# Attention scores in split precision: three 64-row matmuls per map, two maps in turn, instead of two 128-row matmuls on stacked parts

## The chip, the cores and the metric

The kernel runs on one core of a Trainium2 chip. A core has five engines that run side by side: TensorE (matrix products, PE in the profile, with its weight loads as PEld), VectorE (DVE), ScalarE (ACT), GpSimd (POOL) and SyncE (SP), whose queue issues nearly all DMA transfers here. The metric is the device time of one execution in microseconds (us); lower is better. Shown are the times of three runs and one profiled execution.

## The reference

One layer of a residual trunk on 2048 positions of width 1024, in float32:

```
u = rms_norm(h);  proj = u @ W_in            # diff q,k,v | sb q,k,v
# diff attention, 4 heads, two maps c = 0, 1 of 64 columns each, QK-normed
logits = einsum('bqhcd,bkhcd->bhcqk', q, k) * scale + bias   # chunk-causal mask
p = softmax(logits);  attn = p[:, :, 0] - lam * p[:, :, 1];  y_A = attn @ v
# stick-breaking attention, 8 heads of 64 columns, strictly causal
z = einsum('bqhd,bkhd->bhqk', q, k) * scale
log_1mb = where(mask, log_sigmoid(-z), 0)
rem = cumsum(log_1mb, reverse) - log_1mb
a = where(mask, exp(log_sigmoid(z) + rem), 0);  y_B = a @ v
h = h + concat(norm(y_A), norm(y_B)) @ W_out
h = h + (silu(u2 @ W_gate) * (u2 @ W_up)) @ W_down,  u2 = rms_norm(h)
```

Everywhere the contraction of a score is over 64 columns of q and k.

## The kernel before

Every float32 operand of a product is split into a high and a low float16 part, and a product is summed from high x high, high x low and low x high. The work has two parts. The first (pools `ps`, `sp`, `zp`, `pp`) holds the input projection, both attentions and the output projection; the second is the feed-forward network, whose products over blocks are formed in a scheme with seven products.

The first part runs over eight groups `g` of 128 query columns: `g` 0 to 3 are the diff heads, one head with its two maps each; `g` 4 to 7 are the stick-breaking heads, two heads each. "Map" below means either, `m` = 0 or 1; a map has 64 columns. For each group the projection (`proj`, `proj_tile` L315, 24 matmuls of 384 columns for each of 16 row tiles) gives q, k and v of that group. After every four row tiles `proj_batch` (L349) puts q and k, split, into the float16 tile `st` and turns them by DMA into `qT` and `kT`, with positions along the free axis. In `st` the high and low 64 columns of one map lie next to each other, so that after the transpose a map's high part lies on partitions 0 to 63 and its low part on 64 to 127, 128 rows in all. Two more DMAs (L375) copy the two planes of `qT` with the halves exchanged, low above high, into its planes 0 and 1.

Scores are formed for one row tile `i` of 128 queries and up to 512 keys at a time (a chunk), in a PSUM tile `sc` of one bank; there are four such banks. `score_chunk` (L447) issues two matmuls of 128 rows, 128 columns of output partitions and 128 to 512 moving columns: the first gives high x high + low x low, the second, with the exchanged plane, low x high + high x low. For the last chunk of the stick-breaking heads a third one (L451) adds the mask.

In the diff heads `probs` (L463) goes through map 0 and then map 1: VectorE takes each chunk from PSUM to a float32 tile `z4`, with scaling and a running maximum (L484, and L488 with the bias near the diagonal). Then come the exponentials (ScalarE), the combination of both maps (L508), and `split_t` (L399), which splits into float16 halves and transposes by DMA into `aT` for the product with v (`pv`, L454).

In the stick-breaking heads `stage_a` (L541) treats one map of up to 1024 keys: for each chunk, from the last to the first, two sigmoids on ScalarE (L555 into the tile `om`, L556 in place in PSUM), on VectorE a running product from right to left (L558, a scan) and a product (L559) into the tile `be`, and at the end `split_t` of `be`, its high part on ScalarE and its low part on GpSimd (L99). `stage_b` (L566), some units later, forms the product with v. The tiles `om` and `be` come from the pool of nine `z4` tiles (`ZB` = 9); the float16 tiles before and after the transpose come from rings of three and five.

The order in which an engine executes is not that of the source. A scheduler puts the instructions in order, by priorities (`PRI`, L32) and by when their inputs and buffers come free in its own timeline; matmuls of the projection for the next group, of the products with v and of the scores so stand mixed in TensorE's queue. The projection is advanced (`advance`, L709) by the progress of the attention.

`xf` in `out_proj` (L748) uses the buffers of `st` later for rows of x.

Of the kernel before, what the change touches and what calls it, by code (L numbers as in the profile page):

```python
# [11 lines left out]
F32 = mybir.dt.float32  # L12
F16 = mybir.dt.float16
# [47 lines left out]
def block(tc, a, out):  # L61
# [3 lines left out]
    with top:  # L65
# [185 lines left out]
        with ExitStack() as ph1:  # L251
# [82 lines left out]
            @pri("po")  # L334
            def proj_out(g, G, pj, B, j):
                st, v, raw = B
                nv = 1 if g < 4 else 2
                vv = v[:, j, :].rearrange("p (h s e) -> p h s e", h=nv, s=2)
                split_psum(vv[:, :, 0, :], vv[:, :, 1, :], pj[:, 256:384].rearrange("p (h e) -> p h e", h=nv), 128)
                if g < 4:  # L340
                    if pick(A=270, D=335) == "A":
                        ACT.mul(raw[:, j, :], pj[:, :256], 2.0 ** -11)
                    else:
                        DVE.tensor_scalar(raw[:, j, :], pj[:, :256], 2.0 ** -11, None, op0=ALU.mult)
                else:
                    split_psum(st[:, 0:4, j, 0, :], st[:, 0:4, j, 1, :], pj[:, :256].rearrange("p (c e) -> p c e", c=4), 256)

            @pri("pb")
            def proj_batch(g, G, B):  # L349
                st, v, raw = B  # L350
                qT = sp.tile([P, 4, 4, P], F16, tag="qT", bufs=QB, name=nm("qT"))
                kT = sp.tile([P, 2, 4, P], F16, tag="kT", bufs=KB, name=nm("kT"))
                if g < 4:
                    rq = raw[:].rearrange("p t (c e) -> p t c e", e=64)
                    sq = st[:].rearrange("p c t s e -> p (c t s e)")[:, :2048].bitcast(F32)
                    ACT.activation(sq.rearrange("p (t c e) -> p t c e", t=4, c=4), rq, AF.Square)
                    note("A", 950)
                    ss = sm.tile([P, 16], F32, tag="ss", bufs=2, name=nm("ss"))
                    DVE.tensor_reduce(ss[:], sq.rearrange("p (c e) -> p c e", e=64), op=ALU.add, axis=AX.X)
                    rs = sm.tile([P, 16], F32, tag="rs", bufs=2, name=nm("rs"))  # L360
                    rstd(rs[:], ss[:], 2.0 ** -16 / 64, G["epsk"][:])
                    rsb = rs[:].rearrange("p (t c) -> p t c", c=4).unsqueeze(3).to_broadcast([P, 4, 4, 64])
                    DVE.tensor_tensor(rq, rq, rsb, ALU.mult)
                    note("D", 2300)
                    gb = gk[:].unsqueeze(1).unsqueeze(1).to_broadcast([P, 4, 2, 64])
                    tt(rq[:, :, 2:4, :], rq[:, :, 2:4, :], gb, ALU.mult, 512)
                    for o in range(2):
                        src = rq[:, :, 2 * o : 2 * o + 2, :]
                        d = st[:, 2 * o : 2 * o + 2].rearrange("p c t s e -> p t c s e")
                        to16(d[:, :, :, 0, :], src, 512)  # L370
                        tt(d[:, :, :, 1, :], src, d[:, :, :, 0, :], ALU.subtract, 512)
                for T, c in ((qT[:, 2:4], 0), (kT[:], 2)):
                    SP.dma_start_transpose(T.rearrange("p c t n -> p (c t) n"), st[:, c : c + 2].rearrange("p c t s e -> p (c t s e)"))
                for o in (0, 64):
                    SP.dma_start(qT[o : o + 64, 0:2].rearrange("p c t n -> p (c t n)"), qT[64 - o : 128 - o, 2:4].rearrange("p c t n -> p (c t n)"))  # L375
                G["q"].append(qT)
                G["k"].append(kT)
                G["v"].append(v)

            def proj(g, G, fresh=None):  # L380
                for t in range(NT):
# [62 lines left out]
                return (i % k, k)  # L444

            @pri("sc")
            def score_chunk(G, sc, i, q, m, w, cut=False):  # L447
                for o in range(2):
                    PE.matmul(sc[:, : 128 * w].rearrange("p (t n) -> p t n", n=P), lhsT=G["q"][i // 4][:, 2 - 2 * o + m, i % 4, :], rhs=G["k"][q][:, m, 0:w, :], start=o == 0, stop=o == 1)  # L449
# [11 lines left out]
            def diff_attn(g, G):  # L461
                @pri("at")
                def probs(i):  # L463
# [8 lines left out]
                    for m in range(2):  # L472
                        nx = 0
                        for b in range(nb):
                            n = min(1024, L - 1024 * b)
                            z = z4()
                            for c in range((n + 511) // 512):
                                lo, hi = 512 * c, min(512 * c + 512, n)
                                sc = ps.tile([P, 512], F32, tag="sc", bufs=4, name=nm("sc"))
                                score_chunk(G, sc, i, 2 * b + c, m, (hi - lo) // P)  # L480
                                f = min(max(near - 1024 * b - lo, 0), hi - lo)
                                note("D", 1.05 * (hi - lo) + 200)
                                if f > 0:
                                    DVE.tensor_scalar(z[:, lo : lo + f], sc[:, :f], kz_d[:], None, op0=ALU.mult, op1=ALU.max, accum_out=mx[:, m, nx : nx + 1])  # L484
                                    nx += 1
                                if f < hi - lo:
                                    b0 = 1024 * b + lo + f - (i - 1) * 128
                                    DVE.tensor_tensor_reduce(z[:, lo + f : hi], sc[:, f : hi - lo], bias[:, g, b0 : b0 + hi - lo - f], kz_d[:], -3.0e38, ALU.add, ALU.max, mx[:, m, nx : nx + 1])  # L488
                                    nx += 1
                            zs[m].append((b, n, z))  # L490
# [46 lines left out]
            def sb_attn(g, G):  # L537
                last = {}

                @pri("at")  # L540
                def stage_a(i, m, b):  # L541
                    L = (i + 1) * 128
                    n = min(1024, L - 1024 * b)
                    be, om = z4(), z4()
                    if b == i // 8:
                        DVE.memset(om[:, n : n + 1], 8192.0)
                    else:
                        DVE.tensor_copy(om[:, n : n + 1], last[m][:, 0:1])
                    last[m] = om
                    for c in range((n - 1) // 512, -1, -1):  # L550
                        lo, hi = 512 * c, min(512 * c + 512, n)
                        w = hi - lo
                        sc = ps.tile([P, 512], F32, tag="sc", bufs=4, name=nm("sc"))
                        score_chunk(G, sc, i, 2 * b + c, m, w // P, b == i // 8 and hi == n)
                        ACT.activation(om[:, lo:hi], sc[:, :w], AF.Sigmoid, scale=G["nkz"][:])  # L555
                        ACT.activation(sc[:, :w], sc[:, :w], AF.Sigmoid, scale=G["kz"][:])  # L556
                        ov = om[:, lo:hi][:, ::-1]
                        DVE.tensor_tensor_scan(ov, ov, sc[:, :w], om[:, hi : hi + 1], op0=ALU.mult, op1=ALU.bypass)  # L558
                        DVE.tensor_tensor(be[:, lo:hi], sc[:, :w], om[:, lo + 1 : hi + 1], ALU.mult)  # L559
                        note("A", 1.7 * w + 400)  # L560
                        note("D", 3.15 * w + 350)
                    return n, split_t(be[:, :n], n, "A", "P")

                ypd = {}

# [177 lines left out]
            def out_proj():  # L743
                for t in range(NT):
                    mt = pp.tile([P, 2 * D], F16, tag="xt", bufs=3, name=nm("mt"))[:].rearrange("p (k n) -> p k n", k=KT)
                    with tc.high_priority(PRI["wm"]) if PRI["wm"] else nullcontext():
                        mts.append(SP.dma_start(mt, ms[t]))
                    xf = pp.tile([P, 6, 4, 2, 64], F16, tag="st", name=nm("xf"))[:].rearrange("p c t s e -> p (c t s e)").bitcast(F32)[:, :D]  # L748
# [425 lines left out]
```

## Time and profile before

| | |
|---|---|
| Runs before, median (lowest to highest) | 2856.76 us (2854.7 to 2862.01) |
| Profiled execution: its own time | 2849.59 us |
| Profiled execution: span from the first to the last instruction | 2847.8 us |
| Mean granted TensorE clock | 0.957 |
| Score matmuls (L449) | 1280, 347.2 us busy, first and last at about 105 and 1391 us |
| Projection matmuls (L321) | 3072, 576.2 us busy |
| Products with v (L459) | 4896, 281.3 us busy |
| Transfers that exchange the halves of qT (L375) | 64 of 128 KB |

A group of instructions is shown as line, engine, operation, written tile <- read tiles, shapes and count, then its busy time and the mean of one in ns, then the time its engine sat idle just before it and what ended that. A row of busy times by stretch gives the stretch, its length, the busy time and count of each engine, the granted TensorE clock, the share of the DMA engines and GB/s. A timeline row gives start and length in us, engine, line, and how many instructions of a kind followed one another; the length runs to the end of the last one's record. Matmul ends are modelled, and matmuls overlap, so a sum of record lengths is more than the time they took. In the waits, "A <- B" is the time that A sat idle until B released it, with the number of waits and the longest.

### The profile page before, as it was taken

To read this page: it belongs to the slowest core of one execution; us is meant where nothing else is said; L and a number is where in the kernel's file an instruction comes from. 1 tells how busy PE (TensorE), PEld (TensorE's weight loads), DVE (VectorE), ACT (ScalarE), POOL (GpSimd) and SP (SyncE) were. 2 spreads that over 40 slices of the span, in tenths; PEclk is the share of its full clock that TensorE was granted. 3 is DMA by queue.
4 is the path that set the end of the run, shared out by engine and by line. 5 is a ranking of instruction groups with operands and counts; after the bars stand their busy time and mean duration, and the time that the engine had idled before them with its cause. 6 is when DMAs were issued, how large, how long until landed. Compare 5 with 4: busy or idle time off the path is not lost.

```text
span 2847.8 us, 45790 instructions
## 1 busy us (share of the span) xinstructions
PE 2519.3 (88%) x17052; PEld 1409.9 (50%) x17052; DVE 2229.5 (78%) x3922; ACT 1481.5 (52%) x2666; POOL 1703.5 (60%) x1133
## 2 busy tenths in 40 slices
PE   7998898888888777788888999899998999999997
PEld 4565556555555444477763444444443444444443
DVE  6898879787989999787638776877778868678675
ACT  4665656567787888656515443534433324334231
POOL 3577767664545545455627655656666667576663
PEclk9999999999999888999989999999999999999998
DMA  7778887889999898978876434242336442442424
GB/s 235 191 160 177 169 176 168 172 166 219 215 193 197 161 182 162 204 168 226 213 255 181 144 107 163 73 149 97 125 133 238 132 163 84 151 165 74 148 74 177
DMA packets 680094, 469.07 MB, mean 165 GB/s; under 512 B 520688, under 2 KB 610800, under 8 KB 678080
## 3 DMA queue, kind: packets, MB, share of 16 engines
q1 hardware_dynamic: 678048, 464.08, 63.1%
q8 instruction: 133, 2.18, 0.3%
q0 software_dynamic: 512, 1.36, 0.2%
q10 hardware_dynamic: 1312, 0.72, 0.1%
q14 instruction: 89, 0.73, 0.1%
HBM read 239.32 MB, written 90.96 MB: 116 GB/s over the span
## 4 chain that ended last, share of the span: by engine, by line
PE 21%; DVE 16%; DMA 7%; POOL 6%; issue 5%; ACT 3%; SPq 1%; DVEq 0%; POOLq 0%; ACTq 0%
PE pd L1008 11%; DVE wu L215 3%; PE pd L911 3%; POOL fst L99 3%; PE pm L911 3%; PE pa L911 3%; DVE wd L215 2%; DVE cg L99 2%; DMA fst<-in_w_down_dram 2%; DVE cg L976 1%; PE po L757 1%; DVE z L558 1%; DMA aT<-s 1%; DMA xcd<-b 1%; DMA b<-b 1%
## 5 line engine op out<-in xcount | busy, mean ns | idle before, releaser
L99 POOL TENSOR_TENSOR s<-z,s 128x1024 f16<-128x1024 f32 (+7 forms) x288 | 474.5, 1656 | 327.8 <-ACT s L90 299.5
L321 PE MATMUL pj<-w,xt 128*128 128x384 f16 x3072 | 576.2, 336 | 25.7 <-DVE st L331 9.6
L99 POOL TENSOR_TENSOR fst<-fst 128x512 f32<-128x512 f32 x193 | 348.3, 1805 | 225.2 <-DVE wg L215 98.0
L1008 PE MATMUL pd<-wd,act 128*128 128x512 f16 x1848 | 416.2, 384 | 30.0 <-DVE hs L1017 11.2
L321 PEld LDWEIGHTS <-xt 128*128 128x128 f16 x3072 | 301.4, 100 | 238.2 <-issue 45.0
L558 DVE TENSOR_TENSOR_SCAN z<-z,sc 128x512 f32<-128x512 f32 (+3 forms) x320 | 355.6, 1113 | 74.8 <-ACT sc L556 70.6
L449 PE MATMUL sc<-kT,qT 128*128 128x512 f16 (+3 forms) x1280 | 347.2, 362 | 72.7 <-DVE z L559 26.3
L459 PE MATMUL yp<-v,aT 128*128 128x64 f16 (+1 forms) x4896 | 281.3, 207 | 77.1 <-DMA aT<-s 76.2
L459 PEld LDWEIGHTS <-aT 128*128 128x128 f16 x4896 | 244.8, 101 | 168.6 <-DMA aT<-s 105.4
L911 PEld LDWEIGHTS <-wg 128*128 128x128 f16 x1848 | 185.8, 101 | 279.3 <-issue 76.2
L1008 PEld LDWEIGHTS <-act 128*128 128x128 f16 x1848 | 181.4, 99 | 256.6 <-issue 25.0
L911 PEld LDWEIGHTS <-wu 128*128 128x128 f16 x1848 | 182.1, 99 | 231.7 <-issue 19.2
L99 POOL TENSOR_TENSOR hs<-hs,cu 128x512 f32<-128x512 f32 x138 | 190.6, 1391 | 165.4 <-DVE cu L1017 66.4
L90 ACT CAST s<-z 128x384 f16<-128x384 f32 (+7 forms) x216 | 170.4, 790 | 139.2 <-DMA aT<-s 59.0
L1017 DVE SCALAR_TENSOR_TENSOR hs<-pd,c,hs 128x512 f32<-128x512 f32 x192 | 139.0, 745 | 131.0 <-PE pd L1008 98.6
L99 POOL TENSOR_TENSOR act<-cg,act 128x512 f16<-128x512 f32 x108 | 173.2, 1609 | 103.1 <-ACT act L970 103.1
L555 ACT ACTIVATE z<-sc,c 128x512 f32<-128x512 f32 (+3 forms) x320 | 203.8, 637 | 20.4 <-PE sc L449 10.5
L559 DVE TENSOR_TENSOR z<-sc,z 128x512 f32<-128x512 f32 (+3 forms) x320 | 193.3, 606 | 7.7
L556 ACT ACTIVATE sc<-sc,c 128x512 f32<-128x512 f32 (+3 forms) x320 | 196.0, 613 | 0.0
L757 PE MATMUL po<-wo,mt 128*128 128x256 f16 x1536 | 184.2, 279 | 13.0 <-DVE xf L760 12.5
L970 ACT CAST act<-cg 128x512 f16<-128x512 f32 x132 | 80.5, 615 | 212.1 <-DVE cg L976 124.8
L911 PE MATMUL pm<-X,wg 128*128 128x512 f16 x792 | 178.6, 379 | 1.0 <-POOL wg L214 1.0
(228 smaller groups left out, 4480.8 us busy)
## 6 DMA issues: line engine op xcount, KB each, us to landing
xt<-xs SPq DMA_DIRECT2D x112, 512.0 KB, 4.2
hs<-hd SPq DMA_DIRECT2D x96, 512.0 KB, 4.3
hd<-hs SPq DMA_DIRECT2D x80, 512.0 KB, 5.1
fst<-in_w_gate_dram SPq DMA_DIRECT2D x22, 1024.0 KB, 5.1
fst<-in_w_up_dram SPq DMA_DIRECT2D x22, 1024.0 KB, 5.3
fst<-in_w_down_dram SPq DMA_DIRECT2D x22, 1024.0 KB, 4.8
X<-xcd SPq DMA_DIRECT2D x14, 1024.0 KB, 9.6
wst<-in_w_in_dram SPq DMA_DIRECT2D x24, 512.0 KB, 6.5
```

The costliest lines, as they stand in the source:

```text
L90: ACT.copy(dst, src)
L99: (DVE if e == "D" else POOL).tensor_tensor(dst, a_, b_, op)
L321: PE.matmul(pj[:, :384], lhsT=xv[:, xi, kt, :], rhs=G["w"][:, wi, kt, :], start=n == 0, stop=n == 23)
L449: PE.matmul(sc[:, : 128 * w].rearrange("p (t n) -> p t n", n=P), lhsT=G["q"][i // 4][:, 2 - 2 * o + m, i % 4, :], rhs=G["k"][q][:, m, 0:w, ...
L459: PE.matmul(yp[:, y0 : y0 + wd], lhsT=aT[:, a_, :], rhs=v[:, v_ : v_ + wd], start=start and j == 0 and q == 0, stop=stop and j == nb - 1 a ...
L555: ACT.activation(om[:, lo:hi], sc[:, :w], AF.Sigmoid, scale=G["nkz"][:])
L556: ACT.activation(sc[:, :w], sc[:, :w], AF.Sigmoid, scale=G["kz"][:])
L558: DVE.tensor_tensor_scan(ov, ov, sc[:, :w], om[:, hi : hi + 1], op0=ALU.mult, op1=ALU.bypass)
L559: DVE.tensor_tensor(be[:, lo:hi], sc[:, :w], om[:, lo + 1 : hi + 1], ALU.mult)
L757: PE.matmul(po[:, sl], lhsT=mt[:, kt, P * xi : P * xi + P], rhs=wos[2 * h + n][wi][:, kt, :], start=q == 0, stop=q == 23)
L911: PE.matmul(ps_[:].rearrange("p (t n) -> p t n", n=P), lhsT=wv[:, wo, wi, 128 * kt : 128 * kt + 128], rhs=X[xo][:, :, xi, kt, :], start=st ...
L1008: PE.matmul(po[:], lhsT=act[:, ao, xi, 128 * j : 128 * j + 128], rhs=W["d"][:, wo, wi, :], start=start and u == 0 and q == 0, stop=u == nu ...
```

## The change

Scores are formed by three matmuls of 64 rows for each map: high q x high k, low q x high k, high q x low k. The product low x low is no longer formed. For this, `st` now has four planes, q high, q low, k high and k low, each with both maps side by side, 64 columns each. After the transpose map 0 lies on partitions 0 to 63 and map 1 on 64 to 127 in each plane. `qT` has two planes in place of four, and the DMAs that exchanged its halves are gone. `score_pair` takes two score tiles, one for each map, and issues the three products for the two maps in turn, one on the lower and one on the upper half of the partitions. `probs` and `stage_a` ask for both maps of a chunk at once and treat them one after the other; `stage_a` splits both maps at its end. Sizes of pools and rings are as they were.

```diff
                 else:
-                    split_psum(st[:, 0:4, j, 0, :], st[:, 0:4, j, 1, :], pj[:, :256].rearrange("p (c e) -> p c e", c=4), 256)
+                    split_psum(st[:, 0:4:2, j, :], st[:, 1:4:2, j, :], pj[:, :256].rearrange("p (c e) -> p c e", c=2), 256)
...
-                qT = sp.tile([P, 4, 4, P], F16, tag="qT", bufs=QB, name=nm("qT"))
+                qT = sp.tile([P, 2, 4, P], F16, tag="qT", bufs=QB, name=nm("qT"))
...
                     for o in range(2):
-                        src = rq[:, :, 2 * o : 2 * o + 2, :]
-                        d = st[:, 2 * o : 2 * o + 2].rearrange("p c t s e -> p t c s e")
-                        to16(d[:, :, :, 0, :], src, 512)
-                        tt(d[:, :, :, 1, :], src, d[:, :, :, 0, :], ALU.subtract, 512)
-                for T, c in ((qT[:, 2:4], 0), (kT[:], 2)):
-                    SP.dma_start_transpose(T.rearrange("p c t n -> p (c t) n"), st[:, c : c + 2].rearrange("p c t s e -> p (c t s e)"))
-                for o in (0, 64):
-                    SP.dma_start(qT[o : o + 64, 0:2].rearrange("p c t n -> p (c t n)"), qT[64 - o : 128 - o, 2:4].rearrange("p c t n -> p (c t n)"))
+                        src = raw[:, :, 128 * o : 128 * o + 128]
+                        to16(st[:, 2 * o], src, 512)
+                        tt(st[:, 2 * o + 1], src, st[:, 2 * o], ALU.subtract, 512)
+                for T, c in ((qT, 0), (kT, 2)):
+                    SP.dma_start_transpose(T[:].rearrange("p s t n -> p (s t) n"), st[:, c : c + 2].rearrange("p c t e -> p (c t e)"))
...
-                        st = pp.tile([P, 6, 4, 2, 64], F16, tag="st", name=nm("st"))
+                        st = pp.tile([P, 4, 4, P], F16, tag="st", name=nm("st"))
...
             @pri("sc")
-            def score_chunk(G, sc, i, q, m, w, cut=False):
-                for o in range(2):
-                    PE.matmul(sc[:, : 128 * w].rearrange("p (t n) -> p t n", n=P), lhsT=G["q"][i // 4][:, 2 - 2 * o + m, i % 4, :], rhs=G["k"][q][:, m, 0:w, :], start=o == 0, stop=o == 1)
+            def score_pair(G, i, q, w, cut=False):
+                sc = [ps.tile([P, 512], F32, tag="sc", bufs=4, name=nm("sc")) for _ in range(2)]
+                for n, (a_, b_) in enumerate(((0, 0), (1, 0), (0, 1))):
+                    for m in range(2):
+                        h = slice(64 * m, 64 * m + 64)
+                        PE.matmul(sc[m][:, : 128 * w].rearrange("p (t n) -> p t n", n=P), lhsT=G["q"][i // 4][h, a_, i % 4, :], rhs=G["k"][q][h, b_, 0:w, :], start=n == 0, stop=n == 2)
                 if cut:
-                    PE.matmul(sc[:, 128 * w - P : 128 * w], lhsT=idb[:], rhs=tri[:], start=False, stop=True, skip_group_check=True)
+                    for m in range(2):
+                        PE.matmul(sc[m][:, 128 * w - P : 128 * w], lhsT=idb[:], rhs=tri[:], start=False, stop=True, skip_group_check=True)
+                return sc
...
                 @pri("at")
-                def stage_a(i, m, b):
+                def stage_a(i, b):
                     L = (i + 1) * 128
                     n = min(1024, L - 1024 * b)
-                    be, om = z4(), z4()
...
+                    u = [(z4(), z4()) for _ in range(2)]
...
-                        sc = ps.tile([P, 512], F32, tag="sc", bufs=4, name=nm("sc"))
-                        score_chunk(G, sc, i, 2 * b + c, m, w // P, b == i // 8 and hi == n)
...
-                    return n, split_t(be[:, :n], n, "A", "P")
+                        scs = score_pair(G, i, 2 * b + c, w // P, b == i // 8 and hi == n)
+                        for (be, om), sc in zip(u, scs):
...
+                    return n, [split_t(be[:, :n], n, "A", "P") for be, _ in u]
...
                     for b in range(i // 8, -1, -1):
+                        n, aTs = stage_a(i, b)
                         for m in range(2):
-                            n, aT = stage_a(i, m, b)
-                            pend.append((i, m, b, n, aT))
+                            pend.append((i, m, b, n, aTs[m]))
```

In `probs` the loop over the maps moves inside the loop over chunks in the same way.

More of the change, by code (lines that the diff above doesn't have):

```diff
@@ L471, in probs @@
                     mx = sm.tile([P, 2, 8], F32, tag="mx", name=nm("mx"))
[L472 to L478, printed above, removed]
-                                sc = ps.tile([P, 512], F32, tag="sc", bufs=4, name=nm("sc"))
-                                score_chunk(G, sc, i, 2 * b + c, m, (hi - lo) // P)
-                                f = min(max(near - 1024 * b - lo, 0), hi - lo)
+                    nx = 0
+                    for b in range(nb):
+                        n = min(1024, L - 1024 * b)
+                        z = [z4() for _ in range(2)]
+                        for c in range((n + 511) // 512):
+                            lo, hi = 512 * c, min(512 * c + 512, n)
+                            sc = score_pair(G, i, 2 * b + c, (hi - lo) // P)
+                            f = min(max(near - 1024 * b - lo, 0), hi - lo)
+                            k = nx
+                            for m in range(2):
+                                nx = k
                                 note("D", 1.05 * (hi - lo) + 200)
                                 if f > 0:
-                                    DVE.tensor_scalar(z[:, lo : lo + f], sc[:, :f], kz_d[:], None, op0=ALU.mult, op1=ALU.max, accum_out=mx[:, m, nx : nx + 1])
+                                    DVE.tensor_scalar(z[m][:, lo : lo + f], sc[m][:, :f], kz_d[:], None, op0=ALU.mult, op1=ALU.max, accum_out=mx[:, m, nx : nx + 1])
                                     nx += 1
@@ L487, in probs @@
                                     b0 = 1024 * b + lo + f - (i - 1) * 128
-                                    DVE.tensor_tensor_reduce(z[:, lo + f : hi], sc[:, f : hi - lo], bias[:, g, b0 : b0 + hi - lo - f], kz_d[:], -3.0e38, ALU.add, ALU.max, mx[:, m, nx : nx + 1])
+                                    DVE.tensor_tensor_reduce(z[m][:, lo + f : hi], sc[m][:, f : hi - lo], bias[:, g, b0 : b0 + hi - lo - f], kz_d[:], -3.0e38, ALU.add, ALU.max, mx[:, m, nx : nx + 1])
                                     nx += 1
-                            zs[m].append((b, n, z))
+                        for m in range(2):
+                            zs[m].append((b, n, z[m]))
                     ng = sm.tile([P, 2], F32, tag="ng", name=nm("ng"))
@@ L747, in out_proj @@
                         mts.append(SP.dma_start(mt, ms[t]))
-                    xf = pp.tile([P, 6, 4, 2, 64], F16, tag="st", name=nm("xf"))[:].rearrange("p c t s e -> p (c t s e)").bitcast(F32)[:, :D]
+                    xf = pp.tile([P, 4, 4, P], F16, tag="st", name=nm("xf"))[:].rearrange("p c t e -> p (c t e)").bitcast(F32)
                     SP.dma_start(xf, x[t * P : (t + 1) * P, :])
```

28 lines of the change are left out of this document (14 added, 14 removed).

## The prediction

> **What bounds the kernel now.** I read the page's busy times first, then the busy times by stretch. The attention part, in which the changed matmuls lie, runs from about 105 us, the first score matmul, to 1410 us. I cut it at 610 us: the stick-breaking heads ("sb") begin there with their first scan, and before it lie the softmax heads ("diff").
>
> ```profile
> PE 2519.3 (88%) x17052; PEld 1409.9 (50%) x17052; DVE 2229.5 (78%) x3922; ACT 1481.5 (52%) x2666; POOL 1703.5 (60%) x1133
> ...
> core 0: us, PE busy (x) PEld busy (x) DVE busy (x) ACT busy (x) POOL busy (x), PEclk, DMA share, GB/s
> 100.00:200.00 100.00, 95.95 (x729) 60.32 (x728) 90.40 (x289) 64.21 (x173) 64.15 (x50) 1.00 0.80 177
> 105.00:610.00 505.00, 457.19 (x3622) 292.04 (x3620) 431.57 (x1300) 304.78 (x795) 354.39 (x253) 0.98 0.80 172
> 610.00:1410.00 800.00, 657.70 (x6768) 446.48 (x6766) 673.85 (x1177) 587.25 (x1102) 429.98 (x281) 0.93 0.91 192
> ...
> L449 PEld LDWEIGHTS <-qT x1280: 95/98/152, 105.5 to 1390.9; 128*128 128x128 f16 x183
> L558 DVE TENSOR_TENSOR_SCAN z<-z,sc x320: 455/1271/1281, 613.4 to 1396.1; 128x512 f32<-128x512 f32 x88, 128x128 f32<-128x128 f32 x24, 128x256 f32<-128x256 f32 x24, 128x384 f32<-128x384 f32 x24
> ```
>
> In the diff stretch TensorE is busy 457 of 505 us (90%) and idle 48; in its best 100 us it reaches 96%. In the sb stretch it is busy 658 of 800 (82%) and idle 142, and VectorE is a little busier than it (674, 84%). So the first stretch is TensorE's, the second is shared. Next I read what the score matmuls are, by shape, and how tightly TensorE's runs stand in the timeline (start, length, what).
>
> ```profile
> L449 PE MATMUL sc<-kT,qT 128*128 128x512 f16 x896 | 277.4, 394 | 49.9 <-DVE z L559 22.5 <-DVE z L546 11.5 <-DVE z L548 9.3
> L449 PE MATMUL sc<-kT,qT 128*128 128x384 f16 x128 | 33.7, 347 | 5.7 <-DVE z L548 2.8 <-DVE z L546 2.7
> L449 PE MATMUL sc<-kT,qT 128*128 128x256 f16 x128 | 25.5, 284 | 6.3 <-DVE z L546 2.8 <-DVE z L548 2.1 <-DVE z L559 1.2
> L449 PE MATMUL sc<-kT,qT 128*128 128x128 f16 x128 | 20.3, 226 | 10.9 <-DMA kT<-st 3.0 <-DMA qT<-qT 2.7 <-DVE z L559 2.6
> ```
>
> ```profile
> 184.17 0.39 PE L459 MATMUL yp<-v,aT 128*128 128x128 f16 x4
> 184.39 0.38 PE L449 MATMUL sc<-kT,qT 128*128 128x256 f16 x2
> 184.61 0.55 PE L459 MATMUL yp<-v,aT 128*128 128x128 f16 x7
> ...
> 186.57 0.59 PE L449 MATMUL sc<-kT,qT 128*128 128x512 f16 x2
> 187.00 1.46 PE L321 MATMUL pj<-w,xt 128*128 128x384 f16 x8
> 188.30 0.59 PE L449 MATMUL sc<-kT,qT 128*128 128x512 f16 x2
> ...
> 193.00 0.49 PE L449 MATMUL sc<-kT,qT 128*128 128x384 f16 x2
> 193.32 1.14 PE L321 MATMUL pj<-w,xt 128*128 128x384 f16 x6
> ```
>
> A matmul's record (394 ns) is longer than the time it takes from its neighbours: from 186.57 to 187.00 two 512-column ones cost 0.43 us, 0.215 each; 384 columns cost 0.16, 256 columns 0.11, and 128 columns 0.055 (four from 184.17 to 184.39). Weight loads cost nothing beside them. Each record also overlaps the next run by about 0.16 us (186.57 + 0.59 = 187.16, next run at 187.00): the array drains one while it takes in the next.
>
> **The change, part by part.** *The score stream.* Now it is 896 x 0.215 + 128 x (0.16 + 0.11 + 0.055) = 193 + 42 = 234 us, 117 in each stretch (the two kinds of head have the same chunks). The change makes it three matmuls of the same columns in place of two: one after another they take 351 us, +117. They take less only where two on different halves (partitions 0 to 63, 64 to 127) stand next to each other and run side by side. The source alternates the halves, but the instructions are put in order by a scheduler, and in the changed kernel's order on TensorE they mostly do not alternate. The 1920 matmuls stand in 527 runs with other work between them, 246 in diff and 281 in sb, and 456 of the runs are just the three of one map. Only 289 neighbours in all change the half. Letting the second of such neighbours start with the first, as its half is free, saves 32 us over all runs (20 in diff, 12 in sb). So the stream grows by 85 us at least and 117 at most. No row here shows two halves side by side; I take the middle, 101 (49 diff, 52 sb).
>
> By the Trainium skill, TensorE: Matmul & The Clock Gate, Part 3 (Packing small matmuls), matmuls in distinct row groups do run at the same time; by that rule the growth would be 85, and with strict alternation the stream would even shrink to three quarters, about -59 us.
>
> *Changing the array between 128 and 64 rows.* Every run now sits between matmuls of 128 rows, so TensorE's array form changes 2 x 527 = 1054 times, 492 in diff and 562 in sb. The profile has three such excursions, for the bias table's 32-row matmuls; the one at full clock, and for comparison another f32 run that keeps 128 rows:
>
> ```profile
> 32.94 0.67 PE L321 MATMUL pj<-w,xt 128*128 128x384 f16 x3
> 33.55 0.91 PE L634 MATMUL bt<-z,z 32*128 32x384 f32 x2
> 34.38 0.34 PE L321 MATMUL pj<-w,xt 128*128 128x384 f16 x1
> ...
> 761.86 0.60 PE L432 MATMUL yp<-id,y 128*128 128x128 f32 x4
> 762.29 0.65 PE L321 MATMUL pj<-w,xt 128*128 128x384 f16 x3
> ```
>
> Going in, the record before ends at 33.61 and the run starts at 33.55, an overlap of 0.06 in place of 0.16: 0.10 us lost. Going out, 34.46 against 34.38: 0.08 lost. The f32 run of 128 rows overlaps its successor by 0.17, so it is the rows and not the type. At 0.09 each, 1054 changes cost 95 us (44 diff, 51 sb). The bounds are 0, if 64 rows do not behave as 32, and 0.10 each, 105 us. I take 95, the only row there is.
>
> The Trainium skill, TensorEngine Tiling (Array Packing), Key Properties, says that a change of tiling mode drains TensorE, and does not limit that to 32 rows; by it the bound of 0 falls.
>
> *What TensorE's added time does to the end.* Added are 93 us in diff and 103 in sb. Diff: 457 + 93 = 550 us of work in a stretch that is packed to 90% and at best to 96%. At 93%, halfway, it takes 592, so +87. Sb: 658 + 103 = 761; at 96% it would still fit in 800, at today's 82% it would take 926. VectorE holds a bound of its own there, and idle time beside it can fill; I take 92%, which is 827, so +27. Sum +114. The FFN from 1410 us on has no part in the change.
>
> *The swapped copy of q.* Its plane is dropped, and with it 64 transfers on SP's queue:
>
> ```profile
> qT<-qT SPq DMA_DIRECT2D x64, 128.0 KB, 2.5
> ...
> L375 SPq DMA_DIRECT2D qT<-qT x64: 461/587/1224, 75.0 to 1217.2; - x64
> ...
> who waited for it (us, times):
>   PE sc L449: 2.9, 5
>   PEld L449: 2.7, 3
> ```
>
> They hold SP's queue for 64 x 0.59 = 38 us, and TensorE waited for them 5.6 us in all. Between 0 and 6 us of gain; I count 0, since the q transpose before them stays. The transposes stay as many and as large. The new layout of `st` moves no instruction to another engine.
>
> *Two maps in turn.* Score tiles of both maps are requested together, and `stage_a` builds both maps before it splits either, so the splits and their transposes come in twos, and four `z4` tiles are taken at once from a ring of nine. What stands in the way of this today:
>
> ```profile
> L99 POOL TENSOR_TENSOR s<-z,s 128x1024 f16<-128x1024 f32 x120 | 264.5, 2208 | 163.7 <-ACT s L90 148.2 <-issue 6.8 <-DVE m L178 4.2
> L558 DVE TENSOR_TENSOR_SCAN z<-z,sc 128x512 f32<-128x512 f32 x224 | 285.0, 1273 | 40.6 <-ACT sc L556 38.0 <-PE pj L321 1.6
> L559 DVE TENSOR_TENSOR z<-sc,z 128x512 f32<-128x512 f32 x224 | 153.4, 686 | 5.1
> ...
> POOL s L99 <- ACT s L90: 299.5, 136, 11.4
> DVE z L558 <- ACT sc L556: 70.6, 58, 6.8
> ```
>
> VectorE needs 2 x 2 x (1.27 + 0.69) = 7.8 us for a 1024-wide block of both maps, GpSimd 2 x 2.2 = 4.4 for its two splits: one block's splits are done while VectorE does the next. Counted at 0, hidden under those 7.8 us; without that cover it is a rival below, on the one side, and the 70.6 us for which the scan waits for ScalarE are one on the other.
>
> *Sum.* The profiled execution took 2849.6 us (span 2847.8). 2849.6 + 114 = 2964; it lies 7 us under the median of the runs, 2856.8, so the median to expect is 2971, 4% slower.
>
> **The rivals.**
> 1. *TensorE has room.* The halves overlap where they can, changing rows is free, and the rest goes into idle time. Diff: 457 + 39 = 496, at 96% 517, so +12; sb: 658 + 46 = 704 in 800, +0. 2857 + 12 = 2869. For it: 48 + 142 us of idle. Against it: the 0.08 and 0.10 us above.
> 2. *Faster: the scan stops waiting.* With two independent maps in turn, ScalarE has the second map's sigmoids ready while VectorE scans the first, and the 70.6 us before the scan vanish: 2857 - 71 = 2786. It decides only if TensorE's added time is under what it has idle, 190 us, and is issued in time; at my 196 it does not. Against it: diff has no such wait to give back and is TensorE's.
> 3. *The ring makes the blocks wait.* A block's first `om` tile reuses a `be` tile of two blocks earlier, so it waits for that one's split; before, the slack was three maps, now two. GpSimd is busy only 430 of 800 us in sb, but it already waits 299.5 us for ScalarE's half of the split, and ScalarE does that behind its sigmoids. There are 24 blocks in each of four sb groups; if each loses half a split, 1.1 us, that is 96 x 1.1 = 106 us on top: 3077.
>
> **How the numbers follow.** The forecast, 2971, has 0.66; its own bounds are the stream at 85 to 117 and the changes at 0 to 105, with the packing between today's and the best, from rival 1's 2869 to (457 + 59 + 49) / 0.905 = 624 (+119) and (658 + 59 + 56) / 0.822 = 940 (+140) on top of 2857, 3116. Rival 1 has 0.07, of which 0.04 lie within 0.3% (9 us, about what a measurement of this kernel tells from no change) and 0.03 a little above. Rival 2 has 0.06, rival 3 0.21. So faster 0.06, same 0.04, slower 0.90. I cut the range where a tenth is left out on either side: 2880 to 3085.
>
> **What will show it.** In the changed profile: 1920 score matmuls of 64 rows; a start-to-start time of 0.215 us within a run of three of one map; an overlap of records of some 0.07 where a run begins and ends; TensorE's idle share in attention below today's; attention's end near 1520 us with the FFN's length unchanged; the waits for score tiles (VectorE's at L484, ScalarE's at L555) grown. The forecast is wrong if the runs of 64 rows keep the 0.16 us overlap, if matmuls of one half are much shorter than 0.215, or if VectorE's queue rather than TensorE's carries the longer attention.

## The result

The changed kernel takes 2931 us against 2856 us: the ratio is 1.025 (95% interval 1.023 to 1.028), 75 us slower, 4 runs each. The prediction said slower, 2971 us, with 2880 to 3085 as its range: the sign and the range held, and of the forecast's 114 us came 75. Its profiled execution took 2925.6 us (span 2923.6).

To see where the time went I cut each kernel's execution by events: first score matmul, first scan (end of the diff heads), last scan, end. For the kernel before these are at 106, 613, 1396 and 2848 us. For the changed kernel they are read from two lines of the views by line, first and last start:

```profile
L449 PEld LDWEIGHTS <-qT x1920: 92/94/148, 105.0 to 1461.2; 64*128 64x128 f16 x192
L563 DVE TENSOR_TENSOR_SCAN z<-z,sc x320: 451/1270/1282, 661.7 to 1463.5; 128x512 f32<-128x512 f32 x112, 128x128 f32<-128x128 f32 x16, 128x256 f32<-128x256 f32 x16, 128x384 f32<-128x384 f32 x16
```

Busy times by stretch: stretch, its length, then PE, PEld, DVE, ACT, POOL, the granted clock, DMA share, GB/s. First before:

```profile
106.00:613.00 507.00, 459.19 (x3664) 294.33 (x3663) 434.06 (x1305) 307.43 (x799) 354.71 (x254) 0.98 0.80 172
613.00:1396.00 783.00, 642.12 (x6554) 432.43 (x6552) 665.32 (x1162) 578.39 (x1089) 417.60 (x273) 0.93 0.91 191
1396.00:2848.00 1452.00, 1334.22 (x6384) 630.75 (x6381) 1055.43 (x1295) 544.97 (x676) 891.80 (x560) 0.96 0.43 144
```

and after:

```profile
105.00:662.00 557.00, 524.67 (x3917) 277.80 (x3916) 435.75 (x1298) 305.00 (x794) 353.57 (x253) 0.99 0.68 150
662.00:1464.00 802.00, 735.49 (x6937) 437.81 (x6936) 667.79 (x1171) 580.76 (x1094) 418.14 (x273) 0.93 0.88 184
1464.00:2924.00 1460.00, 1333.60 (x6390) 630.94 (x6386) 1053.22 (x1293) 545.94 (x677) 891.66 (x559) 0.96 0.43 143
```

The diff stretch is 50 us longer, the sb stretch 19, the rest 8. VectorE, ScalarE and GpSimd do the same work in both. TensorE is busy 65 us more in diff, which is then packed to 94% (91% before), and 93 us more in sb, packed to 92% (82% before). So most of the added work in diff lengthened it, and most of that in sb went into idle time.

The score matmuls in the groups, and TensorE's timeline (start, length, line, count):

```profile
L449 PE MATMUL sc<-kT,qT 64*128 64x512 f16 (+3 forms) x1920 | 423.9, 362 | 46.5 <-DVE z L564 25.2
```

```profile
179.82 2.60 PE L321 MATMUL pj<-w,xt 128*128 128x384 f16 x15
182.35 1.48 PE L449 MATMUL sc<-kT,qT 64*128 64x512 f16 x12
183.76 0.95 PE L461 MATMUL yp<-v,aT 128*128 128x128 f16 x14
184.65 0.82 PE L449 MATMUL sc<-kT,qT 64*128 64x512 f16 x3
185.40 0.40 PE L461 MATMUL yp<-v,aT 128*128 128x128 f16 x4
185.73 0.50 PE L449 MATMUL sc<-kT,qT 64*128 64x256 f16 x3
```

The group's busy time rose from 347 to 424 us, by 77. But it counts each run to the end of its last record, with the overlap into the next run and the change of rows behind it, so it is not the stream of the prediction. Counted in the trace from each start to the next, with idle time left out, the score matmuls took 259 us before and 389 after, of which the 527 changes behind their runs are 49: the stream grew by 82 us, 33 in diff and 49 in sb. Twelve matmuls that alternate between the halves took 1.41 us from start to next start (182.35 to 183.76), where twelve in a row at 0.215 would take 2.6: two on different halves do run side by side (six pairs at 0.215 are 1.29, and the change of rows behind them 0.09). A run of three of one map took 0.75 (184.65 to 185.40): 3 x 0.215 and 0.10 more, the change behind it. Each record overlaps its neighbour by 0.06 to 0.07 us where the rows change (183.76 + 0.95 = 184.71 against 184.65; 185.47 against 185.40) and not by 0.16: the 0.09 us per change that the 32-row rows of before gave. Over all runs the median change costs 0.092 us on leaving (308 ns from a 512-column matmul to the next start, in place of 216) and 0.095 us on entering (258 ns after a projection matmul, in place of 163).

### The profile page after: what moved, and what is told of

It is laid out like the page before. It is cut to its first block, busy times and chain, and to the rows that moved or that the text cites. A ratio compares the mean times of both kernels' runs of the same rounds, so it can differ in the third digit from the quotient of the medians.

```text
span 2923.6 us, 47071 instructions
## 1 busy us (share of the span) xinstructions
PE 2676.2 (92%) x17692; PEld 1398.6 (48%) x17692; DVE 2230.3 (76%) x3922; ACT 1482.8 (51%) x2666; POOL 1706.1 (58%) x1133
## 4 chain that ended last, share of the span: by engine, by line
PE 26%; DVE 17%; DMA 8%; POOL 6%; issue 5%; ACT 3%; SPq 0%; DVEq 0%; POOLq 0%; ACTq 0%
PE pd L1013 11%; PE pd L916 3%; PE po L762 3%; DVE wu L215 3%; POOL fst L99 3%; PE pa L916 2%; PE pm L916 2%; DVE z L563 2%; DVE wd L215 2%; DMA aT<-s 2%; DVE cg L99 2%; PE sc L449 2%; DMA fst<-in_w_down_dram 1%; DVE cg L981 1%; DMA hs<-hd 1%
## 5 line engine op out<-in xcount | busy, mean ns | idle before, releaser
L99 POOL TENSOR_TENSOR s<-z,s 128x1024 f16<-128x1024 f32 (+7 forms) x288 | 468.6, 1638 | 325.0 <-ACT s L90 268.1
L321 PE MATMUL pj<-w,xt 128*128 128x384 f16 x3072 | 567.8, 332 | 15.1 <-DMA xt<-xs 5.2
L449 PE MATMUL sc<-kT,qT 64*128 64x512 f16 (+3 forms) x1920 | 423.9, 362 | 46.5 <-DVE z L564 25.2
L563 DVE TENSOR_TENSOR_SCAN z<-z,sc 128x512 f32<-128x512 f32 (+3 forms) x320 | 353.1, 1111 | 80.2 <-ACT sc L561 74.5
L321 PEld LDWEIGHTS <-xt 128*128 128x128 f16 x3072 | 288.3, 99 | 245.6 <-issue 76.5
L461 PEld LDWEIGHTS <-aT 128*128 128x128 f16 x4896 | 226.7, 101 | 151.6 <-issue 93.0
L560 ACT ACTIVATE z<-sc,c 128x512 f32<-128x512 f32 (+3 forms) x320 | 204.1, 638 | 41.4 <-PE sc L449 21.8
L449 PEld LDWEIGHTS <-qT 64*128 64x128 f16 x1920 | 119.9, 96 | 207.9 <-issue 64.9
L487 DVE TENSOR_SCALAR_CACHE_REDUCE z<-sc,c 128x512 f32<-128x512 f32 (+3 forms) x256 | 161.7, 649 | 49.6 <-PE sc L449 45.3
```

The source lines that it names most:

```text
L99: (DVE if e == "D" else POOL).tensor_tensor(dst, a_, b_, op)
L321: PE.matmul(pj[:, :384], lhsT=xv[:, xi, kt, :], rhs=G["w"][:, wi, kt, :], start=n == 0, stop=n == 23)
L449: PE.matmul(sc[m][:, : 128 * w].rearrange("p (t n) -> p t n", n=P), lhsT=G["q"][i // 4][h, a_, i % 4, :], rhs=G["k"][q][h, b_, 0:w, :], st ...
L461: PE.matmul(yp[:, y0 : y0 + wd], lhsT=aT[:, a_, :], rhs=v[:, v_ : v_ + wd], start=start and j == 0 and q == 0, stop=stop and j == nb - 1 a ...
```

## The experiments

Each ran beside the kernel before on the same chip; times are medians, ratios are to that kernel with their 95% intervals.

**pairs: the handling of two maps alone.** The changed kernel with the layout, the copies and the 128-row matmuls of before:

```diff
-                for n, (a_, b_) in enumerate(((0, 0), (1, 0), (0, 1))):
-                    for m in range(2):
-                        h = slice(64 * m, 64 * m + 64)
-                        PE.matmul(sc[m]..., lhsT=G["q"][i // 4][h, a_, i % 4, :], rhs=G["k"][q][h, b_, 0:w, :], start=n == 0, stop=n == 2)
+                for m in range(2):
+                    for o in range(2):
+                        PE.matmul(sc[m]..., lhsT=G["q"][i // 4][:, 2 - 2 * o + m, i % 4, :], rhs=G["k"][q][:, m, 0:w, :], start=o == 0, stop=o == 1)
```

> The changed kernel's handling of the two maps (both maps of a chunk asked for together, both split at the end of a block, four z4 tiles at a time) with the score matmuls, the planes of qT and the exchanging DMAs of the kernel before. If TensorE's added time is what made the change slower, this is level with the kernel before, within 0.5% (2842 to 2870). If rival 3 holds (the ring and the bursts of splits make the blocks wait), most of the 75 us is here: 2900 or more. If rival 2 had anything in it (the scan waits less with two maps in turn), it is faster than before by some tens of us, 2785 to 2840.

Measured: 2847 us, ratio 0.9965 (0.9954 to 0.9977). So rival 3 falls: asking for both maps and splitting in twos costs nothing. It came out 10 us faster; the run neutral below shows how little that says.

**rows128: three matmuls, all of 128 rows.**

```diff
-                        h = slice(64 * m, 64 * m + 64)
+                        h = slice(0, P)
```

> The changed kernel with its three score matmuls on all 128 rows in place of 64 (both maps' scores are then the sum over the two maps, so the scores are not the reference's; the work of every other engine is as before). No array form changes, and no two matmuls run side by side: TensorE gets +117 us over the kernel before, against +77 for the stream and 99 for 1054 changes of 64 and 128 rows, 176, in the changed kernel. If the end moves by some 0.43 of TensorE's added time (75 of 176), this gives +50: 2906, faster than the changed kernel by 25. If changes of rows cost nothing at the end and the stream alone counts, it is slower than the changed kernel: 2931 + 0.97 x 40 = 2970 (75 us for 77 us of stream).

Measured: 2902 us, ratio 1.016 (1.014 to 1.018), near the 2906 expected.

```profile
105.00:650.00 545.00, 504.27 (x3919) 317.80 (x3917) 433.49 (x1297) 304.17 (x791) 354.12 (x253) 0.98 0.71 152
650.00:1437.00 787.00, 680.74 (x6925) 459.65 (x6922) 665.27 (x1170) 578.77 (x1096) 420.49 (x273) 0.97 0.90 188
```

TensorE is busy 45 us more than before in diff, and diff is 38 longer; 39 us more in sb, and sb is 4 longer. Without changes of rows, and with nothing side by side, the third matmul is cheaper than in the changed kernel. Luck of the order has no part in this for most of the attention: TensorE executes the same order in both up to 1132 us of rows128. Up to the first scan the changed kernel's TensorE is busy 20 us more and needs 12 us longer; from there to the end of the common order it is busy 27 us more and needs 4 us longer.

**switch and noswitch: changes of rows by themselves.** The kernel before with a small matmul of zeros between the two of each chunk, on 64 rows and, as control, on 128:

```diff
+            zw = sp.tile([P, P], F16, name="zw", bufs=1)
+            DVE.memset(zw[:], 0.0)
...
+                    if o == 1:
+                        PE.matmul(sc[:, :64], lhsT=zw[0:64, :], rhs=zw[0:64, 0:64], start=False, stop=False, skip_group_check=True)
```

In noswitch the operands are `zw[:, :]` and `zw[:, 0:64]`.

> The kernel before, with one small matmul more between the two of each score chunk: 64 rows of zeros by 64 columns, into the same PSUM tile, so that the result stays. Each is an excursion from 128 to 64 rows and back: 640 x (2 x 0.094 + 0.029) = 139 us of TensorE's time, of which 120 are the changes of rows. If the end moves by 0.43 of TensorE's added time it is 60 us over the kernel before: 2917, and 52 over the same kernel with the small matmul on 128 rows. If the changes cost nothing at the end because TensorE would have been idle, it is level with that one.

> The control: the same small matmul on all 128 rows (zeros again), so no change of rows; 640 x 0.029 = 19 us of TensorE's time. At 0.43 of it: +8, 2865; it may be level with the kernel before.

Measured: 2896 us (1.014, 1.011 to 1.017) and 2878 us (1.007, 1.004 to 1.009). Stretches of switch, then of noswitch:

```profile
105.00:655.00 550.00, 527.03 (x3958) 303.63 (x3957) 430.58 (x1303) 306.00 (x796) 355.07 (x255) 0.98 0.75 158
655.00:1437.00 782.00, 697.61 (x6881) 446.90 (x6879) 665.77 (x1164) 579.96 (x1094) 414.23 (x272) 0.94 0.92 193
```

```profile
104.00:624.00 520.00, 470.79 (x3973) 306.94 (x3971) 429.04 (x1304) 306.78 (x797) 358.31 (x254) 0.97 0.81 168
624.00:1415.00 791.00, 651.71 (x6864) 447.18 (x6863) 667.60 (x1164) 578.68 (x1092) 411.50 (x272) 0.92 0.91 190
```

The 1280 changes add 56 us of TensorE's busy time in diff, which becomes 30 us longer, and 46 in sb, which becomes 9 shorter. Here too TensorE's order is the same in both, up to 1199 us of noswitch, so the 30 us are no luck of the order; in the part of sb with the same order switch is busy 37 us more and takes 6 us less. The difference of the medians is 17 us, not the 52 expected from one share for both stretches: in sb these changes were free, in diff they cost about half of their time. The control itself cost 20 us for 19 us of work, more than expected.

**chain: alternation enforced.** An issue order among the six matmuls of a pair:

```diff
-                        PE.matmul(...)
+                        mm.append(PE.matmul(...))
+                        if len(mm) > 1:
+                            tc.add_manual_dep(mm[-1].ins, mm[-2].ins.name, ..., reason="issue order")
```

> The changed kernel with the six score matmuls of a pair bound to alternate between the maps (an issue order among them, no wait), banks as they were. The first one often still stands alone: 534 runs, so the changes of rows stay (1068 x 0.094 = 100 us), but the stream falls from 321 to about 221 us, 14 less than before. TensorE's added time is 86 us in place of 176; at 0.43 of it the end is +37: 2893. If only the changes of rows mattered it would stay at 2931; if only the stream did, it would be level with the kernel before, 2850.

Measured: 2929 us (1.026, 1.024 to 1.029), level with the changed kernel, where 2893 was expected. Stretches, then some of its waits in sb:

```profile
103.00:654.00 551.00, 508.92 (x4005) 273.48 (x4004) 431.39 (x1307) 312.34 (x806) 357.52 (x256) 0.97 0.70 153
654.00:1467.00 813.00, 694.25 (x6908) 427.16 (x6906) 666.92 (x1162) 569.70 (x1080) 408.50 (x270) 0.91 0.86 181
...
DVE z L566 <- ACT sc L564: 87.8, 69, 3.8
PE yp L464 <- DMA aT<-s: 42.2, 35, 3.3
PE sc L450 <- DVE z L567: 34.6, 43, 2.1
```

The two waits of TensorE in sb were these in the changed kernel:

```profile
PE sc L449 <- DVE z L564: 25.2, 29, 4.8
PE yp L461 <- DMA aT<-s: 19.9, 22, 3.2
```

TensorE is busy 16 us less than in the changed kernel in diff and 41 less in sb, but diff is only 6 us shorter and sb is 11 longer: its idle time rose from 32 to 42 and from 66 to 119 us. The order that saves its time makes it wait: in sb its waits for transposed tiles `aT` rose from 20 to 42 us, those for VectorE's last product on a score tile from 25 to 35, and the scan waited for ScalarE 88 us in place of 74.5 (shown below under the rivals).

**onetile and pairs2b: six matmuls together, by one PSUM tile of two banks for both maps.** The same edit in the changed kernel and in the kernel of pairs (the transposes of x, which share these tiles, then also hold one of two banks):

```diff
-                sc = [ps.tile([P, 512], F32, tag="sc", bufs=4, name=nm("sc")) for _ in range(2)]
+                pair = ps.tile([P, 1024], F32, tag="sc", bufs=2, name=nm("sc"))
+                sc = [pair[:, :512], pair[:, 512:]]
```

> The changed kernel with one PSUM tile of two banks for both maps of a chunk (two such tiles in place of four single banks), so that both halves come free together and the six matmuls of a pair stand together: 289 runs in place of 527, the halves alternating. TensorE: stream 176 us (235 in the kernel before), 578 changes of rows x 0.094 = 54, together 5 us less than before. If TensorE's added time is the cause, it is level with the kernel before: 2840 to 2865. If the order of the maps is the cause, it stays near 2930. If banks that come free only in twos hold the scores back, it lies between, with the waits of ScalarE and VectorE for score tiles grown beyond the changed kernel's.

> The kernel of run pairs (128-row matmuls, both maps asked for together) with one PSUM tile of two banks for both maps in place of two of one bank. TensorE's work is that of the kernel before. If banks that come free only in twos are what made the alternating version with a two-bank tile 170 us slower, this is slower too, by 100 us or more: 2950 to 3030. If the 64-row matmuls or their changes of rows made it, this is level with the kernel before.

Measured: onetile 3025 us (1.059, 1.057 to 1.062), pairs2b 3032 us (1.061, 1.059 to 1.063). In onetile's timeline the side-by-side running is plain:

```profile
311.76 0.81 PE L321 MATMUL pj<-w,xt 128*128 128x384 f16 x4
312.51 0.82 PE L450 MATMUL sc<-kT,qT 64*128 64x512 f16 x6
313.26 1.47 PE L321 MATMUL pj<-w,xt 128*128 128x384 f16 x8
```

Six matmuls take the 0.75 us that three take in the changed kernel. Yet the kernel is 94 us slower than the changed one, and with 128-row matmuls the same tile costs 185 us (3032 against the 2847 of pairs), so it is the tile. Stretches of onetile and its waits in sb (engine line waited for: us in total, times, longest), then those of pairs2b:

```profile
113.00:641.00 528.00, 462.09 (x3980) 263.78 (x3979) 427.36 (x1305) 309.41 (x801) 352.23 (x252) 0.97 0.72 155
641.00:1568.00 927.00, 682.90 (x6900) 436.05 (x6898) 681.66 (x1160) 578.22 (x1075) 414.18 (x269) 0.83 0.73 158
...
DVE z L564 <- ACT sc L562: 163.4, 153, 3.2
ACT z L561 <- DVE z L565: 146.4, 110, 3.9
```

```profile
634.00:1575.00 941.00, 700.39 (x6615) 467.89 (x6613) 677.62 (x1162) 587.61 (x1085) 413.84 (x270) 0.84 0.75 160
...
DVE z L566 <- ACT sc L564: 166.5, 123, 7.4
ACT z L563 <- DVE z L567: 79.0, 78, 2.8
```

Diff gains by alternation (528 us, against 557 in the changed kernel), sb loses 125 us: the scan waits for ScalarE 163 us (70.6 in the kernel before), and ScalarE waits for VectorE to finish the last product on a tile. That fits two engines which, with two tiles, no longer run ahead of each other. TensorE, idle for longer, was also granted less of its clock in sb, 0.83 and 0.84 in place of 0.93; how much of the loss that is was not separated.

**nocopy, copyunused and aftercopy: the 64 transfers.** The kernel before without them, both matmuls on the plane that is not exchanged; the same with the transfers kept; and the changed kernel with them put back into planes that nothing reads:

```diff
-                for o in (0, 64):
-                    SP.dma_start(qT[o : o + 64, 0:2]..., qT[64 - o : 128 - o, 2:4]...)
...
-                    ... lhsT=G["q"][i // 4][:, 2 - 2 * o + m, i % 4, :] ...
+                    ... lhsT=G["q"][i // 4][:, 2 + m, i % 4, :] ...
```

> The kernel before without the 64 transfers that exchange the halves of qT; both score matmuls then use the plane that is not exchanged, so the scores lack the mixed products and count the others twice, with the same work on every engine. The prediction counted 0 to 6 us of gain: 2850 to 2857. If SP's queue or the DMA engines bound the attention (their share is 0.87 to 0.92 there), it is more, 2840 or less.

> The kernel before with the 64 transfers, but with both score matmuls on the plane that is not exchanged (so the scores lack the mixed products, as in run nocopy). If the 22 us of nocopy came from the matmuls no longer waiting for the second copy, they are here too: 2836. If they came from the transfers' place on SP's queue and the DMA engines, this is level with the kernel before: 2857. In between, or outside, it is the order of instructions that the scheduler happens on.

> The changed kernel with the 64 transfers of 128 KB put back, into two planes of qT that no matmul reads; the matmuls are the changed kernel's. If taking the transfers away was worth 22 us in the changed kernel too, as run nocopy has it for the kernel before, this is 2931 + 22 = 2953. If nocopy's gain came from its matmuls no longer waiting for the second copy to land, or from a luckier order of instructions, it stays at 2931 (2925 to 2937).

Measured: nocopy 2835 us (0.992, 0.990 to 0.994), copyunused 2860 us (0.999, 0.998 to 1.001), aftercopy 2922 us (1.022, 1.018 to 1.025). Taking the transfers out of the kernel before gained 23 us, more than three times what neutral below moved, and not by the matmuls' waits alone, since copyunused, which does not read the exchanged plane, gained nothing. But putting them into the changed kernel cost nothing; it came out 10 us lower, with overlapping intervals. TensorE's order is another in each of these kernels, so how much of the 23 us is the order is not known. The transfers' worth in this change is between nothing and some 23 us, and stays open.

**neutral: how much the order of instructions alone moves the end.** A spare constant set to zero on VectorE, once per batch:

```diff
+                DVE.memset(spare[:], 0.0)
                 qT = sp.tile([P, 4, 4, P], F16, tag="qT", bufs=QB, name=nm("qT"))
```

> The kernel before with 32 more instructions of one column on VectorE (a spare constant set to zero once per projected batch, some 0.06 us each, 2 us in all), which nothing reads. It shows how much the end moves when the scheduler only comes to another order: if within 0.2% (5 us), the 10 us of run pairs and of aftercopy are effects of their edits; if it moves by 10 us or more, they may be luck of the order.

Measured: 2854 against 2861 us, ratio 0.998 (0.997 to 0.999). Work was added and the kernel came out 7 us faster; in the trace TensorE's order departs from that of before at the 15th matmul. The 7 us lie between the two marks of the expectation, so differences of some 10 us between these kernels, that of pairs among them, are not shown to come from their edits, nor shown to be luck. The profiles give a second measure. In before, pairs, neutral, nocopy and copyunused, whose matmuls have the same shapes and numbers, diff takes 497 to 508 us, sb 776 to 793, and the rest 1452 to 1464. The changed kernel's diff, 557 us, lies far outside; its sb, 802 us, only 9 us beyond.

**solo: one map after the other.** The layout and three 64-row matmuls of the change, with the loops of before:

```diff
+                h = slice(64 * m, 64 * m + 64)
+                for n, (a_, b_) in enumerate(((0, 0), (1, 0), (0, 1))):
+                    PE.matmul(sc[:, : 128 * w]..., lhsT=G["q"][i // 4][h, a_, i % 4, :], rhs=G["k"][q][h, b_, 0:w, :], start=n == 0, stop=n == 2)
```

> The changed layout and the three 64-row matmuls per map, but one map after the other as in the kernel before (score tiles, z4 tiles and splits of one map at a time). By TensorE's time: stream 337 us in place of 321 in the changed kernel, 1096 changes of rows (103 us), 204 over the kernel before in place of 176; 0.43 x 28 = 12 over the changed kernel, and the 10 us that asking for both maps was worth in run pairs are missing: 2953. If the halves standing next to each other matter more than this, it is 2970 or more; if asking for both maps holds 64-row matmuls back, it is faster than the changed kernel, 2925 or less.

Measured: 2940 us (1.029, 1.024 to 1.033), between the changed kernel and the 2953 expected. Its interval overlaps that of the changed kernel: alternating the maps in the source gave little or nothing that can be told from it, as the order on TensorE already said. The 28 us in its expectation mix two measures: the 176 us take the stream by the records' busy time (77), the 204 from start to start. From start to start the difference is 16 us of stream and 4 of changes, 20, and the sum gives 2950.

## Why the prediction was right, and where its sizes were off

*The scheduler undoes the alternation.* Right: TensorE executed mostly runs of three of one map, and solo, which does not alternate at all, is about as fast.

*The stream.* This is the term that was mis-sized: 101 us taken, 82 measured from start to start, about the lower bound of 85. I had taken the middle between running side by side and not, for want of a row. It does run side by side (twelve in 1.41 us). By the Trainium skill, TensorE: Matmul & The Clock Gate, Part 3, that was to be expected, and this trace agrees.

*The changes of rows.* Right in size: 0.09 us for each change, read from the two edges of the one full-clock 32-row excursion, holds for 64 rows (0.092 and 0.095). That one excursion would stand for all of them was an assumption. The rule of the Trainium skill's TensorEngine Tiling, Key Properties, which excluded zero, agrees. What they cost at the end depends on the stretch (switch against noswitch): about half in diff, nothing in sb.

*How TensorE's time reaches the end.* Right in diff, and in sb within what luck allows: packings of 93% and 92% were taken, 94% and 92% came out. With 65 and 93 us more of busy time in place of the 93 and 103 of the sum, diff grew by 50 instead of 87 and sb by 19 instead of 27. The added busy time was overestimated by 38 us, and the smaller stream explains 19. The rest is a term the sum lacked: before each idle spell TensorE's busy time holds some 0.17 to 0.19 us of the last matmul's modelled end, which back-to-back matmuls hide, and the changed kernel has 117 such spells in attention in place of 217, which is 20 us less. Between the stretches, 45 projection matmuls, 7 us, left diff, and 43 came to sb. The 93% was a middle chosen between two packings, so its nearness to 94% is partly luck. In sb the kernels with TensorE's work unchanged scatter by 17 us, nearly the 19 measured, so that 92% came out says little. The 8 us after the last scan were not in the sum, and lie within the scatter of that stretch, 1452 to 1464 us.

*The transfers.* Counted at 0; nocopy has 23 us and aftercopy none. The prediction's bound of 6 us, from TensorE's waits, was too narrow for the kernel before if the 23 us are the transfers'; what else they do there was not found.

*Rivals.* The first (room on TensorE, changes free) is half right in place: sb has the room, diff has not. The second falls: with two maps in turn the scan still waited,

```profile
DVE z L563 <- ACT sc L561: 74.5, 64, 4.5
DVE z L487 <- PE sc L449: 45.3, 66, 5.0
ACT z L560 <- PE sc L449: 21.8, 21, 3.8
```

74.5 us against 70.6; and the waits for score tiles rose as the forecast said, to 45.3 us on VectorE in diff and 21.8 on ScalarE, from these in the waits of the kernel before:

```profile
DVE z L484 <- PE sc L449: 16.7, 18, 2.1
ACT z L555 <- PE sc L449: 10.5, 8, 3.2
```

The second rival was for a kernel in which TensorE's time does not grow, and pairs is one. There the scan's wait did fall, by 20 us,

```profile
DVE z L565 <- ACT sc L563: 50.3, 43, 4.3
```

but sb took 783 us, as before: part of the wait went, and the time did not. The third falls by pairs.

*Still open:* why chain, with TensorE busy 57 us less than the changed kernel in attention, ends no earlier. Part of the answer is that 41 of these are in sb, where TensorE's time decides little: rows128 has 55 us less of it there than the changed kernel, and is 15 us shorter. That chain's sb is 11 us longer than the changed kernel's is of the size of the scatter. That a first matmul of a pair now holds its bank while the second map's bank is still in use fits the rise in TensorE's idle time, and pairs2b shows that banks held in twos are dear in sb; but this was not tested on chain.

Of the versions that compute the same scores none is shown to beat the kernel before: pairs (0.9965) is 10 us faster, and neutral, which only adds work, 7 us.

## What to carry to other kernels

Read the order in which a scheduler places matmuls before counting on two of them running side by side: here most runs held one map, and the pairing was lost. Count each run of partial rows among full-row work with two changes of rows, 0.09 us each, and weigh TensorE's added time by stretch: where it was packed to over 90% half or more of it came through; where it idled beside a VectorE that was busier than it, a fifth or less. Tying two results to one PSUM tile to force the pairing can cost more than the pairing gains, when two engines pass the banks on in turn.

## What was not expected of the hardware

Six 64-row matmuls of 512 columns in alternation take no longer than three in a row on one half, 0.75 us with the change of rows behind them, so the overlap of two halves is complete. And a change of rows that costs TensorE 0.09 us each time can be free at the end: the half of switch's 1280 that lie in sb left that stretch no longer than the control's (782 against 791 us).
